# The second half's first norm and small delta factors emitted ahead of the first half's branches; six modulation units later, two of them beside the expert rows

## Chip, cores and metric

One core of a Trainium2 chip runs the whole program once. The metric is the device time of one execution in microseconds, and the number compared is the median of three executions. Times inside a run come from one profiled execution and are counted from the start of its span.

## What is computed

One transformer block on 512 tokens of width 1024, in float32: a modulation vector from the condition, a token mixer of two recurrent branches (HGRN2 and gated delta net), and a product-key expert layer with 16384 experts, of which each token takes 8 x 16. Cut to what matters here:

```python
mod = (cond @ ada_w[l] + ada_b[l])[:, None, :]
sh1, sc1, gt1, sh2, sc2, gt2 = jnp.split(mod, 6, axis=-1)
h = rmsnorm(x, norm1_g[l]) * (1.0 + sc1) + sh1
y = token_mixer(h, ...)          # projections, two recurrences, two gated branches, w_out
x = x + gt1 * y
h = rmsnorm(x, norm2_g[l]) * (1.0 + sc2) + sh2
x = x + gt2 * peer(h, ...)       # scores over all keys, top 16 per head, weighted sum of expert rows
return rmsnorm(x, final_g)
```

In the mixer `beta_raw` and `a_raw` (8 columns of the projection) give the small factors of the delta net: beta, the log decay and its cumulated exponentials.

## The kernel before

**Halves.** The 512 tokens go through the mixer in two halves of 256. A half is normed and transposed into `hh` and `hl` (`front_norm`, line 806, over `norm_t`, line 232): high and low parts, because every wide product is made of three float32r products (`mm3`, lines 202 to 204). Both lie in a pool with one buffer of each, so those of the second half can be written only when the last product that reads the first half's is done. `gdn_small` (line 262) then makes the small factors: 16 narrow products from `hh` and `hl` (lines 267 and 269), two transposes, and a chain of some 20 tiny DVE operations.

**Weights.** A projection unit is two loads of 512 KB on SP's queue (`half_unit`, line 191), each into one of four buffers named `raw`; ACT casts it to `whi` (line 197), DVE makes `wlo` (line 198), and 48 products on PE read them.

**Modulation units.** The modulation is made in 12 units of 512 columns (`ada_unit`, line 135). A unit loads 4 x 512 KB into the same four `raw` buffers (line 142), sums eight slices on DVE into `adac` (lines 146 and 152) and ends with a product on PE. Units 0 to 3 (shift and scale of the first norm) run at the start. Units 4 and 5 give the gate `gt1`, 6 to 9 shift and scale of the second norm, 10 and 11 the gate `gt2`. A gate's unit loads its bias row (`adar`, line 159), adds the product (line 161) and stores it in DRAM (line 162), from where it is read much later.

**Order of the mixer.** `mixers` (line 825) is a generator: convolutions and projections of the delta net, the inverses in steps of three, the HGRN2 projections, `hgrn_core`, then `gdn_seq` (line 456), the recurrence of the delta net, in four steps one after the other (two pairs of heads by two blocks of 128 tokens). For the first half the gate projections of all branches follow, then a head norm and `branch` for HGRN2 and for the delta net. `run(mixers(0, *h1), ar, ADA[1], ADA[0])` (line 972) puts modulation unit 4 and those after it between its steps: none for the first `ADA[0]` steps, then one after every `ADA[1]` steps, 6 and 2. After it come `front_norm` for the second half, four steps of `back0` (the output projection of the first half, `mix_out`, line 867), and `mixers(1)` with the rest of `back0` beside it.

**Expert layer.** Three token blocks go through dense products over all experts, the fourth through gathered expert rows. In `dense` (line 1181) item i is one block of 128 experts: `value_parts` (line 1109) loads 512 KB of values through the same `raw` buffers, `wlo` on DVE (line 1003), the 192 KB of scores `gr` from DRAM (line 1117), times the gates `g` (line 1121), split into `ah` and `al` (lines 1124, 1125); then 18 products into `y`. Every eighth item loads the next 1.5 MB of gates (line 1113). Scores of the first 32 items were made ahead. `gather_block` (line 1136) runs beside it, with `rows` gathered by GpSimd and summed on DVE.

**What sets the order.** The framework's scheduler orders the instructions of each engine, by the order of emission and a timeline that it assumes; each engine then runs its own list strictly in that order. What is written earlier gets precedence, but instructions far apart in the code lie side by side on an engine.

Of the kernel before, what the change touches and what calls it, by code (L numbers as in the profile page):

```python
# [11 lines left out]
F32 = mybir.dt.float32  # L12
# [8 lines left out]
P = 128  # L21
# [23 lines left out]
GB = 3  # L45
NGS = 5
NST = 4
ADA = (6, 2)
ND = 384
AHEAD = 32  # L50
LEAD = 3
# [15 lines left out]
def mixer_peer_kernel(ctx: ExitStack, tc: tile.TileContext, x, ws, ada, wba, vecs, rows, skt, uv, ut, out, dbg=None):  # L67
# [17 lines left out]
    def bank(tag):  # L85
        return (psh if tag == "hg" else ps).tile([P, 512], F32, tag=tag, name=tag, bufs=psb[tag])
# [4 lines left out]
    def w2(tag, shape=(P, 2, 256), dt=F32, bufs=1, name=None):  # L91
        pool = wka if tag in WKA else wkb if tag in WKB else wk
        return pool.tile(list(shape), dt, tag=tag, name=name or tag, bufs=bufs)
# [38 lines left out]
    a1 = cst.tile([P, KD], F32, name="a1")  # L132
    a2 = cst.tile([P, KD], F32, name="a2")

    def ada_unit(u, first=False):

        pp = bank("tr")
        acc = w2("ac", (P, 512), bufs=2, name="adac")
        parts = []
        for i in range(4):  # L140
            w = st.tile([P, 2, 512], F32, tag="raw", name="adaw")
            nc.sync.dma_start(w, ada[u, :, 2 * i:2 * i + 2])
            for a in range(2):
                kk = 2 * i + a
                if kk == 0:
                    nc.vector.tensor_scalar(acc, w[:, 0, :], cond[:, 0:1], None, op0=ALU.mult)
                elif first and a:
                    p = w2("gs", (P, 512), bufs=NGS, name="adap")
                    nc.scalar.mul(p, w[:, a, :], cond[:, kk:kk + 1])
                    parts.append(p)  # L150
                else:
                    nc.vector.scalar_tensor_tensor(acc, w[:, a, :], cond[:, kk:kk + 1], acc,
                                                   op0=ALU.mult, op1=ALU.add)
        parts.append(acc)
        if u // 2 in (2, 5):
            dst, o = (g1d, RW_B1) if u < 6 else (g2d, RW_B2)
            k = u % 2 * 512
            r = w2("ac", (P, 512), bufs=2, name="adar")
            nc.sync.dma_start(r, bass.AP(tensor=rows.tensor, offset=rows.offset + o + k, ap=[[0, P], [1, 512]]))
            nc.tensor.matmul(pp, ones, acc, start=True, stop=True)  # L160
            nc.vector.tensor_add(r, r, pp)
            nc.sync.dma_start(dst[:, k:k + 512], r)
            return
        for n, p in enumerate(parts):
            for c in range(4):
                nc.tensor.matmul(pp[:, c * P:(c + 1) * P], p[:, c * P:(c + 1) * P], ones, start=n + c == 0,
                                 stop=n == len(parts) - 1, skip_group_check=True)
        m = mod[:, 4 * u:4 * u + 4]
        nc.vector.tensor_add(m, pp.rearrange("p (c n) -> p c n", c=4)[:, :, 0],
                             vec[:, VC_ADAB + 4 * u:VC_ADAB + 4 * u + 4])  # L170
        if u // 2 in (1, 4):
            dst, g = (a1, VC_N1) if u < 6 else (a2, VC_N2)
            k = u % 2 * 4
            nc.vector.scalar_tensor_tensor(dst[:, k:k + 4], m, 1.0, vec[:, g + k:g + k + 4], op0=ALU.add, op1=ALU.mult)
# [443 lines left out]
    def gate_sig(p, gu, js, hh, hl):  # L618
        r = []
        for j in js:  # L620
            s = gate_tile(p, "gsig")
            nc.scalar.activation(s, proj_tm(gu + j, hh, hl), AF.Sigmoid)
            r.append(s)
            yield
        return r
# [164 lines left out]
                next(aux, None)  # L790

    def ada_rest():
        for u in range(4, 12):
            ada_unit(u)
            yield

# [25 lines left out]
                next(aux, None)  # L822
            yield

    def mixers(p, hh, hl):
        fac = gdn_small(hh, hl)
        yg = w2("yg", (P, 2, 512))
        yh = w2("yh", (P, 2, 512))
        loc = [gdn_pre(0, (yield from gdn_convs(0, fac, hh, hl)))]
# [14 lines left out]
        if p == 0:  # L844
            sg[0] = yield from gate_sig(p, U_GH, range(4), hh, hl)
            gg = yield from gate_proj(p, U_GG, RW_GDN, hh, hl)
            sg[1] = yield from gate_sig(p, U_GD, range(4), hh, hl)
        yhi, ylo = head_norm_t(yh, gh)
        if "yh" in dbg:
            nc.sync.dma_start(dbg["yh"].rearrange("(t p) c -> p t c", p=P)[:, 2 * p:2 * p + 2], yh)  # L850
        if p == 0:
            mg = [w2(n, name="mg") for n in ("hv", "att", "he", "rl")]
        else:
            y2 = w2("yh", (P, 2, 2, 256), name="mg2")
            mg = [y2[:, 0], y2[:, 1]] + [w2("ac", bufs=2, name="mg") for _ in range(2)]
# [68 lines left out]
    h1 = front_norm(0, xc)  # L924
# [44 lines left out]
    ar = ada_rest()  # L969
    RT = dict(side="right", reuse_waits="tile")  # L970
    with tc.tile_pool(name="g0", bufs=1, **RT) as early_gates:
        mg = run(mixers(0, *h1), ar, ADA[1], ADA[0])

    per = ctx.enter_context(tc.tile_pool(name="per", bufs=1, **RT))
    dhi = per.tile([P, KD, ND], F32R, name="dhi")
    dlo = per.tile([P, KD, ND], F32R, name="dlo")
    run(ar)
    h1 = front_norm(1, load_x(1))
    bk = back0(mg)
    for _ in range(4):  # L980
        next(bk)
    mg = run(mixers(1, *h1), bk)
    run(bk)
    c_wa.close()

# [195 lines left out]
    def dense():  # L1181
        for i in range(P - NEND):
            v = value_parts(i)
            for b in range(ND // P):
                for hf in range(2):
                    value_sum(i, b, hf, *v)
            if AHEAD <= i + LEAD < P:
                scores(i + LEAD)
            if i >= 20 or i % 2:
                yield  # L1190
            if i >= AHEAD - LEAD and i % 3 == 0:
                yield
# [84 lines left out]
```

## Time and profile before

| | us |
|---|---|
| median of 3 executions | 1919.0 |
| lowest and highest | 1909.81, 1921.65 |
| the profiled execution, whole | 1918.66 |
| its span | 1916.6 |
| PE (matmul) busy in the span | 1848.3 |
| DVE busy | 1565.6 |
| ACT busy | 966.8 |

The whole time of the profiled execution is 2.1 us more than its span and within 0.4 us of the median. PE is TensorE's matmuls, PEld its weight loads, DVE VectorE, ACT ScalarE, POOL GpSimd, SP the queue on which all plain loads and stores are issued. A row of a timeline gives start, duration, engine, line, operation and tiles, and in brackets the idle time of the engine just before and what ended it. PEclk is the granted clock of TensorE as a share of 2.4 GHz; 0.5 is 1.2 GHz. In order of time: modulation units 0 to 3 (to 37 us), the first half's mixer (to 317), the second half's with the rest of the first half beside it (to 700), routing, gates and early scores (to 954), then the dense expert layer to the end.

### The profile page before, as it was taken

What the parts mean: (1) busy time and instruction counts of PE and PEld (TensorE: products, weight loads), DVE (VectorE), ACT (ScalarE), POOL (GpSimd) and SP (SyncE); (2) the same over time, 40 slices, a digit from 0 to 9 for tenths busy, and PEclk for the clock granted to TensorE, in tenths of its full rate; (3) what the DMA queues carried; (4) which work ended last, traced back from release to release, by engine and by line L of the source; (5) the groups of instructions that cost most, each with busy time, mean ns of one, the idle gap of its engine ahead of it and who ended that gap; (6) DMA issues with size and microseconds to landing.
All of it is one profiled execution on the core that took longest, in us unless ns stands there. A gap on an engine that the chain in (4) does not pass through costs nothing.

```text
span 1916.6 us, 31296 instructions
## 1 busy us (share of the span) xinstructions
PE 1848.3 (96%) x11441; PEld 1709.3 (89%) x11441; DVE 1565.6 (82%) x3422; ACT 966.8 (50%) x1723; POOL 422.3 (22%) x433
## 2 busy tenths in 40 slices
PE   7989998999999899999999999999999999999997
PEld 6989887999989889999987799899899899899896
DVE  5989766889999989999755987878777778788755
ACT  5667544676655688788333333333333333333332
POOL 1010000000000587796100332221122222112100
PEclk9999998999999999999999999999999999999999
DMA  9556663543345555656897998888988998889843
GB/s 312 171 174 193 231 216 119 181 152 115 100 139 157 180 186 195 223 187 246 259 307 208 335 384 319 316 291 314 328 313 306 327 327 282 321 311 327 299 127 110
DMA packets 160521, 459.45 MB, mean 240 GB/s; under 512 B 12528, under 2 KB 78192, under 8 KB 140912
## 3 DMA queue, kind: packets, MB, share of 16 engines
q1 hardware_dynamic: 141936, 323.23, 51.3%
q0 software_dynamic: 18432, 134.23, 18.4%
q8 instruction: 90, 1.47, 0.3%
q14 instruction: 63, 0.52, 0.1%
HBM read 420.71 MB, written 36.70 MB: 239 GB/s over the span
## 4 chain that ended last, share of the span: by engine, by line
PE 81%; DVE 8%; ACT 4%; DMA 4%; POOL 2%; issue 1%; SPq 0%; DVEq 0%; POOLq 0%; ACTq 0%
PE y L203 9%; PE y L204 9%; PE y L202 9%; PE hg L203 9%; PE hg L202 9%; PE hg L204 9%; PE pj L203 6%; PE pj L204 6%; PE pj L202 6%; PE gd L1050 3%; DVE wlo L198 2%; POOL oj L1037 1%; DMA adaw<-in_ada 1%; DMA gr<-sd 1%; DMA raw<-in_ws 1%
## 5 line engine op out<-in xcount | busy, mean ns | idle before, releaser
L1003 DVE TENSOR_TENSOR wlo<-raw,whi 128x1024 fp32r<-128x1024 f32 x256 | 313.1, 1223 | 123.3 <-ACT whi L1002 120.6
L1002 ACT CAST whi<-raw 128x1024 fp32r<-128x1024 f32 x256 | 267.9, 1047 | 241.4 <-PE y L204 222.2
L202 PE MATMUL hg<-dlo,whi 128*128 128x384 f32 x1024 | 348.0, 340 | 1.5 <-ACT ga L1016 1.5
L203 PE MATMUL hg<-dhi,wlo 128*128 128x384 f32 x1024 | 348.1, 340 | 0.0
L204 PE MATMUL hg<-dhi,whi 128*128 128x384 f32 x1024 | 347.5, 339 | 0.0
L1141 POOL DMA_INDIRECT rows<-in_uv,ei x128 | 169.9, 1327 | 737.8 <-DVE acc L1149 571.3
L203 PE MATMUL y<-whi,al 128*128 128x512 f32 x768 | 304.7, 397 | 3.0 <-DVE al L1125 2.9
L204 PE MATMUL y<-whi,ah 128*128 128x512 f32 x768 | 304.4, 396 | 0.0
L202 PE MATMUL y<-wlo,ah 128*128 128x512 f32 x768 | 295.1, 396 | 0.0
L1037 POOL TENSOR_SCALAR oj<-iof,tj 128x128 f32<-128x128 f32 x256 | 213.3, 850 | 55.9 <-PE gd L1050 36.7
L198 DVE TENSOR_TENSOR wlo<-raw,whi 128x1024 fp32r<-128x1024 f32 x160 | 195.5, 1222 | 33.7 <-ACT whi L197 33.3
L197 ACT CAST whi<-raw 128x1024 fp32r<-128x1024 f32 x160 | 167.6, 1049 | 108.3 <-PE pj L204 66.2
L202 PEld LDWEIGHTS hg<-dlo,whi 128*128 128x128 f32 x1024 | 192.2, 188 | 6.3 <-ACT ga L1016 2.2
L1016 ACT ACTIVATE ga<-hg 128x384 f32<-128x384 f32 x128 | 63.0, 492 | 266.9 <-PE hg L204 266.8
L203 PEld LDWEIGHTS hg<-dhi,wlo 128*128 128x128 f32 x1024 | 192.2, 188 | 4.2
L204 PEld LDWEIGHTS hg<-dhi,whi 128*128 128x128 f32 x1024 | 192.2, 188 | 0.0
L203 PEld LDWEIGHTS y<-whi,al 128*128 128x128 f32 x768 | 144.6, 188 | 36.1 <-DVE al L1125 5.4
L204 PEld LDWEIGHTS y<-whi,ah 128*128 128x128 f32 x768 | 144.5, 188 | 34.7
L202 PEld LDWEIGHTS y<-wlo,ah 128*128 128x128 f32 x768 | 144.5, 188 | 31.2 <-ACT ah L1124 0.3
L1154 DVE SCALAR_TENSOR_TENSOR rows<-rows,h2g 128x1024 f32<-128x1024 f32 x128 | 153.9, 1220 | 0.4 <-DMA rows<-in_uv,ei 0.4
L204 PE MATMUL pj<-whi,hh 128*128 128x256 f32 x448 | 129.1, 288 | 0.0
L202 PE MATMUL pj<-wlo,hh 128*128 128x256 f32 x448 | 129.1, 288 | 0.0
(745 smaller groups left out, 3876.7 us busy)
## 6 DMA issues: line engine op xcount, KB each, us to landing
raw<-in_ws SPq DMA_DIRECT2D x160, 512.0 KB, 4.1
raw<-in_ut SPq DMA_DIRECT2D x128, 512.0 KB, 6.1
raw<-in_uv SPq DMA_DIRECT2D x128, 512.0 KB, 5.9
adaw<-in_ada SPq DMA_DIRECT2D x48, 512.0 KB, 4.8
gd<-stage SPq DMA_DIRECT2D x24, 1024.0 KB, 4.6
g<-gd SPq DMA_DIRECT2D x15, 1536.0 KB, 12.3
sd<-ga SPq DMA_DIRECT2D x32, 192.0 KB, 2.8
gr<-sd SPq DMA_DIRECT2D x32, 192.0 KB, 3.9
```

What stands on the lines that cost most here:

```text
L197: nc.scalar.copy(hi, w)
L198: nc.vector.tensor_sub(lo, w, hi)
L202: nc.tensor.matmul(o, lh, rl, start=start, stop=False, **kw)
L203: nc.tensor.matmul(o, ll, rh, start=False, stop=False, **kw)
L204: return nc.tensor.matmul(o, lh, rh, start=False, stop=stop, **kw)
L1002: nc.scalar.copy(hi, w)
L1003: nc.vector.tensor_sub(lo, w, hi)
L1016: nc.scalar.activation(a, o[:, :ND], AF.Gelu)
L1037: (nc.gpsimd if a < npool else nc.vector).tensor_scalar(oj4[:, a, :], iof, tj[:, t0 + a:t0 + a + 1], None, op0=ALU.is_equal)
L1050: last["pe"] = nc.tensor.matmul(pb4(pp, a), oj4[:, a, :], oi4[:, a, :], start=True, stop=True)
L1141: nc.gpsimd.indirect_dma_start(out=r[c], out_offset=None, in_=uv, in_offset=bass.IndirectOffsetOnAxis(ap=ei[:, c:c + 1], axis=0))
L1154: dot = nc.vector.scalar_tensor_tensor(u, u, 1.0, h2, op0=ALU.mult, op1=ALU.mult, accum_out=s)
```

## The change

- `ADA` becomes (12, 2): the units between the first half's steps begin after the twelfth step, and there are six of them (4 to 9).
- Units 10 and 11 are emitted in `dense`, after items 8 and 16, with `adac` and `adar` in the pool `d3` and the product in a bank named `hg`.
- `load_x(1)`, `front_norm(1)` and `gdn_small` of the second half are emitted inside `mixers(0)`, after the last gate projection and ahead of the head norms and branches. `mixers` takes the small factors as an argument.

The number of products, loads and DVE operations stays as it was.

```diff
-ADA = (6, 2)
+ADA = (12, 2)
...
-    def ada_unit(u, first=False):
-
-        pp = bank("tr")
-        acc = w2("ac", (P, 512), bufs=2, name="adac")
+    def ada_unit(u, first=False, pool=None):
+        def work(name):
+            return w2("ac", (P, 512), bufs=2, name=name) if pool is None else pool.tile([P, 512], F32, tag=name, name=name)
+
+        pp = bank("tr") if pool is None else None
+        acc = work("adac")
...
-            r = w2("ac", (P, 512), bufs=2, name="adar")
+            r = work("adar")
...
+            pp = bank("hg") if pp is None else pp
...
-        for u in range(4, 12):
+        for u in range(4, 10):
...
-    def mixers(p, hh, hl):
-        fac = gdn_small(hh, hl)
+    def mixers(p, hh, hl, fac, done=None):
...
             sg[1] = yield from gate_sig(p, U_GD, range(4), hh, hl)
+            done()
         yhi, ylo = head_norm_t(yh, gh)
...
-        mg = run(mixers(0, *h1), ar, ADA[1], ADA[0])
+        nxt = []
+
+        def next_half():
+            h = front_norm(1, load_x(1))
+            nxt.extend((*h, gdn_small(*h)))
+
+        mg = run(mixers(0, *h1, gdn_small(*h1), next_half), ar, ADA[1], ADA[0])
...
     run(ar)
-    h1 = front_norm(1, load_x(1))
     bk = back0(mg)
...
-    mg = run(mixers(1, *h1), bk)
+    mg = run(mixers(1, *nxt), bk)
...
             if AHEAD <= i + LEAD < P:
                 scores(i + LEAD)
+            if i in (8, 16):
+                ada_unit(10 + i // 16, pool=d3)
```

Three places show what the scheduler makes of it. Lines of the changed kernel are a few higher than those of before: 194 is 199, 142 is 146, 159 is 163, 162 is 167.

SP's queue in the first half, before, from the last loads of units 0 to 3 (the twelve `adaw` are three of them); `raw` are weights, `adaw` modulation weights:

```order
L142 DMA adaw<-in_ada 128x1024 x12
L194 DMA raw<-in_ws 128x1024 x3
...
L194 DMA raw<-in_ws 128x1024 x12
L142 DMA adaw<-in_ada 128x1024 x4
L194 DMA raw<-in_ws 128x1024 x4
L142 DMA adaw<-in_ada 128x1024 x4
L159 DMA adar<-in_rows 128x512
L162 DMA g1d<-adar 128x512
L159 DMA adar<-in_rows 128x512
L194 DMA raw<-in_ws 128x1024 x4
```

The same place now:

```order
L146 DMA adaw<-in_ada 128x1024 x12
L199 DMA raw<-in_ws 128x1024 x3
...
L199 DMA raw<-in_ws 128x1024 x24
L146 DMA adaw<-in_ada 128x1024 x2
L163 DMA adar<-in_rows 128x512
L146 DMA adaw<-in_ada 128x1024 x2
L199 DMA raw<-in_ws 128x1024 x4
L146 DMA adaw<-in_ada 128x1024 x3
L167 DMA g1d<-adar 128x512
```

Twelve weight loads (six units) that stood behind modulation units 4 to 6 now stand ahead of unit 4; from there on the units follow each other after every four weight loads, as before.

PE near the end of the first half, before: a step of the delta net's recurrence (lines 460, 467, 472, 478, 484, in this order in a step) among gate projections (`pj` from `hh` and `hl`), with the next step begun behind it:

```order
L203 MATMUL pj<-whi,hl 128x256
L467 MATMUL gd<-r,Xt 128x128 x2
L472 MATMUL gd<-gst,qT 128x128 x2
L204 MATMUL pj<-whi,hh 128x256
...
L614 MATMUL hg<-ident,yh 128x128 x8
L478 MATMUL gd<-z,kd 128x128 x2
L484 MATMUL gd<-z,aq 128x128 x2
L460 MATMUL gd<-gst,kT 128x128 x2
L202 MATMUL pj<-wlo,yhi 128x512 x3
```

Now, behind the first branch's last product (a step is lines 465, 472, 477, 483, 489; 272 and 274 are the narrow products of `gdn_small`, eight of each):

```order
L209 MATMUL pj<-whi,yhi 128x512
L465 MATMUL gd<-gst,kT 128x128 x2
L472 MATMUL gd<-r,Xt 128x128 x2
L477 MATMUL gd<-gst,qT 128x128 x2
L483 MATMUL gd<-z,kd 128x128 x2
L489 MATMUL gd<-z,aq 128x128 x2
...
L272 MATMUL gd<-hh,wb 16x256
L274 MATMUL gd<-hl,wb 8x256
...
L280 MATMUL gd<-ident,ba 128x16 x2
L619 MATMUL hg<-ident,yg 128x128 x8
```

Three of the four steps stand back to back, with no wide product between; the narrow products follow, and then the transposes of the delta net's output `yg`.

DVE in the dense stage, before, from item 8's `gr` (12010) to item 9's `al` (12045):

```order
L1121 TENSOR_TENSOR gr_12010<-gr_12010,g_12008 128x384
L1003 TENSOR_TENSOR wlo_12005<-raw_12002,whi_12004 128x1024
L1121 TENSOR_TENSOR gr_12041<-gr_12041,g_12008 128x384
L1125 TENSOR_TENSOR al_11959<-gr_11955,ah_11958 128x384
L1003 TENSOR_TENSOR wlo_12038<-raw_12035,whi_12037 128x1024
L1125 TENSOR_TENSOR al_12014<-gr_12010,ah_12013 128x384
...
L1125 TENSOR_TENSOR al_12045<-gr_12041,ah_12044 128x384
```

Now, from unit 10's third sum to item 9's `al` (12022; `wlo_12015` is item 9's too, `al_11968` item 8's):

```order
L156 SCALAR_TENSOR_TENSOR adac_11989<-adaw_11994,cond_104,adac_11989 128x512
L1014 TENSOR_TENSOR wlo_11959<-raw_11956,whi_11958 128x1024
...
L156 SCALAR_TENSOR_TENSOR adac_11989<-adaw_11998,cond_104,adac_11989 128x512 x2
L1136 TENSOR_TENSOR al_11968<-gr_11964,ah_11967 128x384
L156 SCALAR_TENSOR_TENSOR adac_11989<-adaw_12002,cond_104,adac_11989 128x512
L1132 TENSOR_TENSOR gr_12071<-gr_12071,g_11962 128x384
L156 SCALAR_TENSOR_TENSOR adac_11989<-adaw_12002,cond_104,adac_11989 128x512
L1014 TENSOR_TENSOR wlo_12015<-raw_12012,whi_12014 128x1024
L1136 TENSOR_TENSOR al_12022<-gr_12018,ah_12021 128x384
```

The low part of item 9's values now waits in DVE's list behind the unit's last sum, and with it behind the unit's last load.

## Rows read from the trace of the kernel before

**Rows 1.** The page, part 1: busy us, share of the span, instructions.

```profile
PE 1848.3 (96%) x11441; PEld 1709.3 (89%) x11441; DVE 1565.6 (82%) x3422; ACT 966.8 (50%) x1723; POOL 422.3 (22%) x433
```

**Rows 2.** Windows: stretch, length, busy of each engine (instructions), PEclk, DMA share, GB/s.

```profile
core 0: us, PE busy (x) PEld busy (x) DVE busy (x) ACT busy (x) POOL busy (x), PEclk, DMA share, GB/s
...
80.00:140.00 60.00, 52.42 (x370) 48.03 (x369) 50.17 (x109) 40.75 (x88) 6.07 (x5) 0.89 0.49 154
140.00:220.00 80.00, 78.34 (x677) 77.71 (x676) 72.13 (x132) 55.76 (x94) 0.00 (x0) 1.00 0.65 209
220.00:240.00 20.00, 16.15 (x112) 15.83 (x111) 15.29 (x27) 7.41 (x9) 2.07 (x1) 0.83 0.69 228
...
280.00:320.00 40.00, 31.24 (x150) 23.36 (x149) 29.15 (x69) 19.10 (x42) 3.04 (x3) 0.87 0.35 111
320.00:540.00 220.00, 220.00 (x1874) 218.56 (x1873) 202.18 (x632) 148.29 (x269) 9.78 (x7) 1.00 0.44 137
...
955.00:1045.00 90.00, 90.00 (x386) 72.35 (x385) 45.17 (x59) 31.93 (x44) 2.61 (x3) 1.00 0.83 267
```

**Rows 3.** Timeline of PE, narrow windows: four waits of the first half.

```profile
88.28 1.28 PE L518 MATMUL hg<-hq,hk 128*128 128x128 f32 x8 [2.70 <-ACT hq L503]
...
115.93 1.50 PE L355 MATMUL gd<-rl,gt 128*128 128x512 f32 x2 [2.67 <-DVE rl L353]
...
233.18 2.07 PE L442 MATMUL gd<-X,al 128*128 128x128 f32 x8 [3.85 <-ACT X L438]
...
292.49 2.59 PE L614 MATMUL hg<-ident,yg 128*128 128x128 f32 x8 [6.42 <-DVE yg L600]
```

**Rows 4.** Timeline of SP's queue, 66 to 125 us.

```profile
69.95 7.88 SPq L142 DMA_DIRECT2D adaw<-in_ada  x4
83.66 11.66 SPq L194 DMA_DIRECT2D raw<-in_ws  x4
97.74 7.49 SPq L142 DMA_DIRECT2D adaw<-in_ada  x4
...
119.60 3.66 SPq L194 DMA_DIRECT2D raw<-in_ws  x2
```

**Rows 5.** Instructions of the tile adaw: ns min/median/max, and its loads.

```profile
L152 DVE SCALAR_TENSOR_TENSOR adac<-adaw,cond,adac x68: 732/746/755, 11.3 to 249.6; 128x512 f32<-128x512 f32 x68
...
DMA to landing us min/median/max: 3.7/4.8/5.8
```

**Rows 6.** Timeline 264 to 273 us: a step of the recurrence among other work.

```profile
264.61 0.61 PE L460 MATMUL gd<-gst,kT 128*128 128x128 f32 x4
...
265.25 0.61 DVE L463 SCALAR_TENSOR_TENSOR r<-gd,neb,vr 128x128 f32<-128x128 f32 x2 [0.45 <-PE gd L460]
...
267.87 0.60 PE L467 MATMUL gd<-r,Xt 128*128 128x128 f32 x4
268.31 0.61 PE L472 MATMUL gd<-gst,qT 128*128 128x128 f32 x4
268.51 0.42 DVE L469 COPY z<-gd 128x256 f32<-128x256 f32 x1 [0.48 <-PE gd L467]
...
270.76 0.61 DVE L480 SCALAR_TENSOR_TENSOR gst<-gst,eb,gd 128x128 f32<-128x128 f32 x2 [1.83 <-PE gd L478]
```

**Rows 7.** Timelines of POOL and DVE, 284 to 298 us: the two norms.

```profile
289.37 1.64 POOL L126 TENSOR_TENSOR rsh<-rs,mhalf 128x8 f32<-128x8 f32 x1 [64.04 <-DVE rs L125]
...
291.81 0.16 DVE L240 TENSOR_REDUCE ssq<-ssq 128x2 f32<-128x8 f32 x1 [2.52 <-ACT junk L238]
```

**Rows 8.** Instructions of the tile mod: the norm's eight activations per half.

```profile
L254 ACT ACTIVATE h<-hg,mod,a x32: 544/563/598, 31.2 to 691.3; 128x256 f32<-128x256 f32 x32
```

**Rows 9.** Timeline of SP's queue, 1000 to 1013 us.

```profile
1001.69 0.37 SPq L1113 DMA_DIRECT2D g<-gd  x1
1002.26 5.02 SPq L1117 DMA_DIRECT2D gr<-sd  x1
1007.37 0.38 SPq L999 DMA_DIRECT2D raw<-in_uv  x1
```

**Rows 10.** Instructions of the tile raw, 955 to 1045 us: its loads.

```profile
DMA to landing us min/median/max: 3.9/4.0/11.2
```

**Rows 11.** Windows: a stretch with idle time on PE at full clock.

```profile
540.00:560.00 20.00, 17.66 (x131) 16.24 (x131) 18.70 (x73) 8.79 (x20) 1.64 (x1) 1.00 0.45 128
```

## The prediction

> **What bounds the kernel now.** I read the page's busy shares first: PE is busy 96% of the span [rows 1], so the time is PE's work, its holes, and what the clock takes away. The profiled execution took 1918.66 us and the median is 1919.0, so every sum below starts at 1918.66 and needs no correction. Within 1% (19 us) is about what a measurement of this kernel can tell from no change.
>
> Then the windows, to find the holes in the stretches that the change touches [rows 2]. From 80 to 140 us PE is busy 52.42 of 60 us at a granted clock of 0.89; from 220 to 240, 16.15 of 20 at 0.83; from 280 to 320, 31.24 of 40 at 0.87. Between them, 140 to 220 has 78.34 of 80 at full clock, and 320 to 540 is full, 220.00 of 220. The dense stage is full on PE too (90.00 of 90), with DVE at only 45.17. So what can be won lies in three places of the first half, and whatever is added to the dense stage must fit beside a PE that never waits.
>
> A window's loss has two parts: idle time, and busy time that runs at less than full clock, (1 − clock) × busy:
> - 80 to 140: 7.58 + 0.11 × 52.42 = 5.8, together 13.4 us.
> - 220 to 240: 3.85 + 0.17 × 16.15 = 2.7, together 6.6 us.
> - 280 to 320: 8.76 + 0.13 × 31.24 = 4.1, together 12.8 us.
>
> PE's timeline gives the waits behind these: 2.70 us for `hq`, 2.67 for `rl`, 3.85 for `X`, 6.42 for `yg` [rows 3]. They are short chains through ACT and DVE which projections would cover if their weights were there. SP's queue shows why they were not: four unit loads at 69.95, four weight loads at 83.66, four unit loads at 97.74 [rows 4]. From 69.95 to 97.74, 27.8 us, four weight loads came, which is two projections. A projection is 48 products, and a product takes 220.00 / 1874 = 0.117 us in the full stretch [rows 2], so two feed PE for 11.2 us of those 27.8.
>
> **Part by part.**
>
> *Units later (80 to 140).* Twelve more weight loads go ahead of unit 4, so the two blocks of unit loads in that stretch leave it, and DVE loses two units' 16 sums of 0.746 us there, 12 us [rows 5], in a stretch in which it is busy 50.17 of 60. With weights at hand the stretch should look like the next, 140 to 220, which loses 1.66 us in 80, or 1.2 in 60: 13.4 − 1.2 = 12.2. The chains of `hq` and `rl` stay, and I keep one short wait of about 1 us: −11. Bounds: −13.4 (all of it) and −4 (the two waits, 5.4 us, go, and alternation that begins within the stretch brings back a part).
>
> *The units that remain (220 to 240).* Six units still follow each other after every four weight loads, and two fewer have to end before the recurrence. I take away the wait of 3.85 and leave the clock: −4. Bounds −6.6 and 0; DVE is busy 15.29 of 20 there, so a wait for it may stay.
>
> *Norm, factors and recurrence (280 to 320).* This is what the emission moves. What goes: the wait for `yg` (6.42), before which the second half's squares on ACT stood; DVE itself waited 2.52 us for their `junk` [rows 7]. They now lie far earlier. What comes is a recurrence without cover. One step is a chain: product, `r`, product, `z`, product, `gst`, or 0.61 + 0.61 + 0.60 + 0.42 + 0.61 + 0.61 = 3.46 us [rows 6] (line 478's product counted like line 472's). PE issues five pairs in it, 0.44 us apart (267.87 to 268.31), 2.2 us. So a bare step leaves 1.3 us idle; three of them, 3.8. Behind the last step come the output's `yg` (0.42, as `z`), four squares (an estimate, 1.7, four of that size), small DVE work (0.6), the power on POOL (1.64 [rows 7]) and a scaling (0.42): 4.8 us, of which 16 narrow products cover 16 × 0.117 = 1.9, leaving 3.0. The norm's `hh` can be written only behind the last gate projection: eight activations of 0.563 us [rows 8] less eight transposes, 4.5 − 1.0 = 3.5. With the clock's 4.1 as now, the stretch would lose 3.8 + 3.0 + 3.5 + 4.1 = 14.4 instead of 12.8: +1.6. So I expect one long wait to be exchanged for many short ones, with no gain. Bounds: −8.8 (all idle goes) and +8 (a wait of 6.42 comes on top).
>
> Whether many short waits keep the clock down is open. The rows have waits of 2.70, 2.67, 3.85 and 6.42 us in windows whose clock is 0.89, 0.83 and 0.87, and a stretch (540 to 560) with 17.66 us busy of 20 and the clock at 1.00 [rows 2, 3, 11]. So 2.3 us of holes in 20 do not lower it; many holes with little work between them are in no row.
>
> The Trainium skill ("TensorE: Matmul & The Clock Gate", section "A second HAM failure mode: psum-queue depth-cycling") says that short idles between groups of products, if frequent enough, make the clock go back and forth. By that rule the bare recurrence and the narrow products would run at half clock from end to end; the sum it gives stands with the first rival.
>
> *Units 10 and 11 in the dense stage.* Their two products are moved, not added: 0. Their 16 sums, 16 × 0.746 = 12 us [rows 5], fit into DVE's 45 idle us of that stage. What can hurt is the order: the low part of item 9's values, and the same place at item 16, waits in DVE's list behind the unit's last sum, and so behind its last load. `raw` loads there land in 4.0 us as a rule, but one took 11.2 [rows 10], 7.2 late; SP itself was held 5.02 us at `gr` behind the issue of the 1.5 MB of gates `g` [rows 9]. Bounds: 0, and one such meeting in full, 7.2 + 5.0 = 12. Values are loaded some items ahead, so I take half of one hold: +2.5.
>
> *The rest, 320 to 954.* The same work with one norm fewer in it; 320 to 540 is full and can't gain. 0, ± 5 (a wait of `yg`'s kind more, or less).
>
> **Sum.** −11 − 4 + 1.6 + 2.5 = −10.9; 1918.66 − 10.9 = 1907.8, about 1908 us.
>
> **Rivals.**
>
> *First: the holes only move.* The six units still pass the same four `raw` buffers, and their alternation now meets the gate projections, the inverses' end and the recurrence. A second loss of the size of 220 to 240, +6.6 in place of −4, gives −11 + 6.6 + 1.6 + 2.5 = −0.3: 1918 us. For it: SP's alternating blocks [rows 4] go on unchanged, only later. Against it: 140 to 220, where units alternated too, lost 1.66 us only [rows 2]. The same sum comes from another mechanism: 16 narrow products and three steps of five pairs, all at half clock, double 1.9 + 6.6 = 8.5 us, of which the 4.1 already counted is a part, and the next products run slow with them for about as long as the stretch 220 to 240 paid, 2.7; 8.5 − 4.1 + 2.7 = 7, on −10.9, is −4: 1915 us. This is what the skill's rule above would do here.
>
> *Second: nearly all is kept.* The stretch 80 to 140 as full as the next (−12.2), 220 to 240 without loss (−6.6), the tail behind the recurrence and the clock's fall avoided (14.4 − 3.0 − 4.1 = 7.3 in place of 12.8, −5.5), nothing lost in the dense stage: −24.3, 1894 us. For it: the fullness of 140 to 220 and 320 to 540. Against it: a bare recurrence, which no row shows running full.
>
> *Third, slower: the dense stage stalls.* Each unit's last load falls behind the gates' 1.5 MB: 7.2 late, 5.0 held on SP, two sums 1.5, so 13.7 us, at item 9 and at item 16, and the clock falls with each (2.7, as in 220 to 240): 2 × 16.4 = 33 on −13.4 for the other terms, 1938 us. It decides from the point at which the two stalls together exceed 13.4, some 6.7 us each. For it: the landing of 11.2 and the hold of 5.02 [rows 9, 10]. Against it: every other item has no such load in its way, PE never waited there, and value loads run ahead.
>
> That the change does not do what it says can be left out: the lists of SP, PE and DVE show it.
>
> **How the numbers follow.** Forecast 0.48 (its own range 1900 to 1916), holes that only move 0.24 (1912 to 1924), nearly all kept 0.20 (1888 to 1900), stalls in the dense stage 0.08 (1925 to 1945). The range 1892 to 1926 leaves out about a third of the second rival and nearly all of the third, some 0.15, and a little for what I did not see. Faster by over 1% (below 1899.5) takes nearly all of the second rival and little of the forecast: 0.22. Slower by over 1% (above 1937.9) is half of the third rival and some unforeseen: 0.07. Within 1%: 0.71.
>
> **What would show it.** Right: SP issues 24 weight loads before unit 4; PE's idle time from 80 to 140 is 1 to 3 us and its clock there 0.95 or more; the place of the 6.42 us wait holds three bare steps with idle times near 1.3 us; PE stays full in the dense stage but for 1 to 3 us about items 9 and 16; DVE's waits there are for `adaw`. Wrong: waits near 3.85 us at `X` or in the gates with a clock below 0.9 (first rival), a recurrence at half clock (its second form), a first half that ends 20 us or more earlier (second), PE waits over 6 us at `y` in the dense stage (third).

## The result, and the profile after

The changed kernel takes 1901.15 us (median of 6 executions, 1898.40 to 1902.23) against 1915.3 for the kernel before (6 executions, 1909.81 to 1921.65): ratio 0.9928, interval 0.9911 to 0.9945, 0.7% faster. The forecast was 1908. The profiled execution took 1898.62 us (span 1896.7), 20 us less than the profiled one of before; the medians are 14 apart. Of the 6 us between these two figures, 3.4 are the old kernel's, whose profiled execution, 1918.66, lies near the top of its spread, and 2.5 the new one's, whose profiled execution lies below its median. Single executions carry a few microseconds of that kind in every comparison of traces below; the comparisons of kernels rest on ratios.

The page, part 1, of the kernel after (busy us, share, instructions); compare [rows 1]:

```profile
PE 1844.5 (97%) x11441; PEld 1708.1 (90%) x11441; DVE 1565.9 (83%) x3422; ACT 972.9 (51%) x1726; POOL 421.5 (22%) x433
```

The work is the same. What changed is where PE waits. Windows of after, with the columns of [rows 2]:

```profile
80.00:140.00 60.00, 57.56 (x472) 55.39 (x471) 49.38 (x103) 48.22 (x89) 3.30 (x3) 1.00 0.53 168
140.00:220.00 80.00, 78.12 (x667) 76.95 (x666) 73.64 (x139) 63.88 (x118) 3.30 (x3) 1.00 0.63 200
220.00:240.00 20.00, 20.00 (x174) 20.00 (x173) 17.37 (x34) 8.79 (x15) 2.07 (x1) 1.00 0.80 268
240.00:280.00 40.00, 34.28 (x196) 28.20 (x194) 26.29 (x67) 16.91 (x45) 3.36 (x2) 0.91 0.37 120
280.00:320.00 40.00, 36.58 (x226) 33.35 (x225) 26.43 (x57) 16.61 (x26) 0.53 (x1) 0.87 0.37 119
...
955.00:1045.00 90.00, 88.15 (x371) 69.19 (x370) 59.88 (x89) 29.84 (x43) 3.15 (x2) 1.00 0.88 281
```

A window's loss, as in the prediction, is its idle time plus (1 − clock) × busy. From 80 to 140 us it has gone from 13.3 us (13.4 in the prediction's rounding) to 2.4, and from 220 to 240 it has gone altogether. But 240 to 280, which was nearly full before, now loses 5.7 idle and 3.1 by the clock. SP's queue shows why the early stretch is full (start, duration, line, transfer, count):

```profile
61.80 42.59 SPq L199 DMA_DIRECT2D raw<-in_ws  x14
108.55 3.60 SPq L146 DMA_DIRECT2D adaw<-in_ada  x2
```

Weight loads run on until 104 us with no unit load between them, and the first unit load stands at 108.55; before, unit loads stood at 69.95 and 97.74 [rows 4]. PE's timeline around the recurrence shows what took the place of the long wait for `yg` [rows 3]. Lines 465, 472, 483 and 489 are the recurrence's, 619 the transposes:

```profile
254.00 0.61 PE L489 MATMUL gd<-z,aq 128*128 128x128 f32 x4
...
261.22 0.75 PE L472 MATMUL gd<-r,Xt 128*128 128x128 f32 x4 [1.49 <-DVE r L468]
...
262.95 0.85 PE L483 MATMUL gd<-z,kd 128*128 128x128 f32 x4 [0.53 <-DVE z L474]
...
266.17 1.22 PE L472 MATMUL gd<-r,Xt 128*128 128x128 f32 x4 [0.45 <-DVE r L468]
...
268.96 1.23 PE L489 MATMUL gd<-z,aq 128*128 128x128 f32 x4
...
278.14 0.33 PE L619 MATMUL hg<-ident,yg 128*128 128x128 f32 x1 [1.53 <-DVE yg L605]
...
298.31 0.80 PE L207 MATMUL pj<-wlo,dhi 128*128 128x256 f32 x2 [3.27 <-ACT dhi L620]
```

Three things are to be seen. The bare steps wait 0.4 to 1.5 us at a time for DVE. The same four passes of line 489 take 0.61 us at 254 and 1.23 at 268.96: the clock has gone to its lower level, 1.2 GHz, with no wait above 1.49 us ahead of it. And the output projection has a wait of 3.27 us for `dhi` that the kernel before did not have.

### The profile page after: what moved, and what is told of

Its sections match the earlier page's. It is cut to its first block, busy times and chain, and to the rows that moved or that the text cites. A ratio compares the mean times of both kernels' runs of the same rounds, so it can differ in the third digit from the quotient of the medians.

```text
span 1896.7 us, 31316 instructions
## 1 busy us (share of the span) xinstructions
PE 1844.5 (97%) x11441; PEld 1708.1 (90%) x11441; DVE 1565.9 (83%) x3422; ACT 972.9 (51%) x1726; POOL 421.5 (22%) x433
## 4 chain that ended last, share of the span: by engine, by line
PE 91%; ACT 3%; DMA 2%; DVE 2%; POOL 1%; issue 1%; SPq 0%; DVEq 0%; POOLq 0%; ACTq 0%
PE hg L208 9%; PE hg L209 9%; PE hg L207 9%; PE y L208 9%; PE y L209 9%; PE y L207 9%; PE pj L207 8%; PE pj L208 8%; PE pj L209 8%; PE gd L1061 3%; PE hg L543 1%; POOL oj L1048 1%; PE gd L453 1%; PE gd L447 1%; PE pj L1061 1%; DMA adaw<-in_ada 1%
## 5 line engine op out<-in xcount | busy, mean ns | idle before, releaser
L1048 POOL TENSOR_SCALAR oj<-iof,tj 128x128 f32<-128x128 f32 x256 | 218.7, 871 | 49.7 <-PE gd L1061 32.6
```

Of the source, the lines that this page charges most:

```text
L1048: (nc.gpsimd if a < npool else nc.vector).tensor_scalar(oj4[:, a, :], iof, tj[:, t0 + a:t0 + a + 1], None, op0=ALU.is_equal)
```

## The experiments

**How a stretch is read.** As in the prediction, a window's loss is its idle time plus (1 − clock) × busy, worked out from the window's row. Three stretches are compared: 80 to 140 us (where the first units were), 140 to 240, and 240 to 320 (recurrence, second branch, start of the output projection). The stretches are fixed in time, and the same work lies earlier in a faster kernel (the transposes of `yg` begin at 292 us in before and at 278 in after). The table has the kernel before, profiled twice, and all other combinations of the three parts of the change:

| kernel | starts after step | units 10, 11 | norm | median us | ratio, 95% | loss 80:140 | 140:240 | 240:320 |
|---|---|---|---|---|---|---|---|---|
| before | 6 | first half | late | 1915.3 | 1 | 13.3 | 8.3 | 13.9 |
| before_again | 6 | first half | late | 1915.52 | 1.0001 (0.9988 to 1.0015) | 13.8 | 4.4 | 13.9 |
| ada_only | 12 | first half | late | 1917.0 | 1.0009 (0.9996 to 1.0022) | 1.8 | 3.7 | 26.1 |
| dense_only | 6 | dense | late | 1909.19 | 0.9969 (0.9954 to 0.9984) | 14.1 | 1.7 | 13.9 |
| front_only | 6 | first half | early | 1906.55 | 0.9967 (0.9949 to 0.9985) | 11.0 | 5.5 | 9.9 |
| no_front | 12 | dense | late | 1902.62 | 0.9937 (0.9915 to 0.9959) | 2.7 | 2.2 | 16.5 |
| ada_front | 12 | first half | early | 1911.36 | 0.9978 (0.9963 to 0.9993) | 1.4 | 2.1 | 20.4 |
| dense_front | 6 | dense | early | 1908.52 | 0.9969 (0.9955 to 0.9984) | 14.0 | 4.0 | 6.8 |
| after | 12 | dense | early | 1901.15 | 0.9928 (0.9911 to 0.9945) | 2.4 | 1.9 | 16.9 |

Ratios are to runs of the kernel before on the same chip. The losses are of one profiled execution each, and one clock fall more or less moves them by about 3 us.

**before_again.** No edit: the kernel before, profiled once more.

> The kernel before, unchanged, profiled once more. Theory: the clock falls at the waits for hq, rl, X and yg (near 89, 116, 232 and 290 us of the span) come from the order of the work and return in every execution; the spread of the times of before (1909.8 to 1921.7) then has another source, such as the start; time 1910 to 1921, the same four falls. Rival: the falls differ from one execution to the next, and the spread is theirs: of the four one or two are missing, and the profiled time is some 6 to 8 us lower than the first profile's 1918.7.

The time is that of before. The windows from 80 to 140 and from 280 to 320 us have their clocks of 0.89 and 0.87 again; the fall at 220 to 240 us did not come back. Its window (columns as above):

```profile
220.00:240.00 20.00, 16.85 (x137) 15.97 (x136) 17.54 (x31) 7.42 (x9) 2.07 (x1) 1.00 0.72 248
```

PE idles 3.15 us there at a clock of 1.00; in the first profile it was 3.85 at 0.83 [rows 2]. So falls do differ between executions (the rival). The two profiled executions differ by 6.2 us: 3.9 of them in the window 140 to 240 and 2.7 in the early dense stage, where PE idles 2.88 us from 955 to 1075 us in the first and 0.16 in the second. What makes the executions differ stays open.

**ada_only**: the later start alone.

```diff
-ADA = (6, 2)
+ADA = (12, 2)
```

> Only the step from which the modulation units begin is changed, 12 for 6; all eight units stay between the first half's steps, and norm, small factors and dense stage are as before. Theory (the gain is the emptied stretch from 80 to 140 us): that stretch loses 2 to 3 us instead of 13.4, and since the two units more have to go somewhere before the first half ends, the loss near 220 to 240 us stays: about -10 us, 1905 on a before of 1915. Rival (the holes only move): eight units behind the twelfth step are too many, a wait of 4 us or more with a clock fall appears between 140 and 300 us for each one saved, and the time is within 3 us of before.

No gain: the rival. The early stretch is emptied as forecast, 13.3 to 1.8, and the recurrence's stretch grows by about the same amount, 13.9 to 26.1. The window of ada_only there:

```profile
240.00:320.00 80.00, 60.52 (x334) 49.20 (x333) 54.97 (x119) 30.39 (x69) 2.92 (x3) 0.89 0.50 167
```

Two waits on PE's timeline in that stretch:

```profile
270.65 0.71 PE L465 MATMUL gd<-gst,kT 128*128 128x128 f32 x4 [2.15 <-DVE gst L485]
...
276.69 1.22 PE L483 MATMUL gd<-z,kd 128*128 128x128 f32 x4 [2.72 <-DVE z L474]
```

DVE's timeline at the second of them (line 156 is a unit's sum, 474 the copy that the step waits for):

```profile
275.55 0.75 DVE L156 SCALAR_TENSOR_TENSOR adac<-adaw,cond,adac 128x512 f32<-128x512 f32 x1 [2.79 <-DMA adaw<-in_ada]
276.22 0.42 DVE L474 COPY z<-gd 128x256 f32<-128x256 f32 x1
```

The copy of `z` stands in DVE's list behind a sum that waits 2.79 us for its load. The last two of eight units now meet the recurrence, and the recurrence stands bare, because the gate projections that used to lie between its steps have gone ahead: the last product from the first half's `hh` starts at 243.6 us and the recurrence's first at 243.0, where before they start at 269.1 and 241.6.

**dense_only**: only units 10 and 11 moved.

```diff
-        for u in range(4, 12):
+        for u in range(4, 10):
...
+            if i in (8, 16):
+                ada_unit(10 + i // 16, pool=d3)
```

> Only units 10 and 11 are moved into the dense stage; the other six begin after step 6 as before, norm and small factors as before. Theory (their place in the first half is worth something by itself): the wait for X and the clock fall near 232 us go, the dense stage pays about 0.6 us: -3 to -5 us, 1910 to 1912 on a before of 1915. Rival (it only pays when the units also begin later): the emptied place is taken by the same waits, within 2 us of before.

The theory, and a little more than it said: 0.9969, some 6 us. The window 140 to 240 loses 1.7 us in place of 8.3 and 4.4 in the two profiles of before; the other two stretches are as they were.

**front_only**: only the norm and the small factors moved.

```diff
+            done()
...
-    h1 = front_norm(1, load_x(1))
...
-    mg = run(mixers(1, *h1), bk)
+    mg = run(mixers(1, *nxt), bk)
```

> Only the emission of the second half's norm and small factors ahead of the branches; modulation units as before (eight, from step 6 on). Theory (one long wait for many short ones): the wait of 6.4 us for yg goes, the bare recurrence and a wait of about 3 us for dhi come, with the clock down for some 17 us in place of 10: +1 to +4 us, 1916 to 1919 on a before of 1915; the losses at 80 to 140 and 220 to 240 us stay as before. Rival (the emission is worth a good part of the gain): -5 us or better, 1910 or less.

The rival: 6 us faster by the ratio, where the theory had 1 to 4 slower. The window of the recurrence is fuller than before:

```profile
240.00:320.00 80.00, 73.06 (x488) 65.97 (x487) 58.69 (x130) 36.21 (x68) 3.81 (x3) 0.96 0.55 178
```

The wait for `yg` is gone, and with the units where they were the steps still have gate projections between them. The early norm does not bare the recurrence. The wait for `dhi` is here too, 3.79 us. Of the 6 us, 4.0 are in this stretch (13.9 to 9.9).

**no_front**: `ADA = (12, 2)` and the dense units, without the early norm.

> Both changes to the modulation units (begin after step 12, units 10 and 11 in the dense stage), without the early norm and small factors. Theory: -11 (80 to 140 us), -6.6 (220 to 240 us), +0.6 in the dense stage, the wait for yg of 6.4 us with its clock fall stays: -15 to -17 us, 1899 on a before of 1915, so 2 us or so faster than the whole change. Rival: the early norm carries part of the gain, and this kernel is 4 us or more slower than the whole change, 1905 or above.

0.9937: between the two. Its recurrence is bare too (16.5 us lost from 240 to 320), with the norm at its old place; and `yg` waits 4.36 us. The early norm on top is worth 0.9937 to 0.9928, which the intervals do not tell from nothing.

**dense_front**: the whole change with `ADA = (6, 2)`.

> The whole change but for the start of the units, which stays after step 6. Theory (the early norm is worth 8 us where gate projections still stand between the recurrence's steps, and beginning later takes them away): the losses from 80 to 140 us stay (about 13 us), the steps of the recurrence are covered by projections, idle time among them under 2 us: 1903 to 1906 on a before of 1915, 2 to 5 us slower than the whole change. Rival (the parts simply add, the later start being worth nothing as it was alone): 1901 or less, no slower than the whole change.

The theory, a little worse: 1908.52, about 7 us above the whole change. The recurrence's stretch is the fullest of all, level with every_1 below; the window of dense_front:

```profile
240.00:320.00 80.00, 74.65 (x522) 68.22 (x521) 55.64 (x124) 40.63 (x74) 3.80 (x3) 0.98 0.47 148
```

It gains 10 us on after there and loses 11.6 from 80 to 140 and 2 from 140 to 240. That is 3.6 of the 8.8 us between the two profiled executions. The rest is from 540 to 700 us (the second half's end): 19.8 us lost against 14.5 in after. The windows of after, dense_front and ada_front, in this order:

```profile
540.00:700.00 160.00, 150.03 (x1112) 141.39 (x1112) 149.27 (x394) 104.29 (x180) 73.69 (x88) 0.97 0.53 172
540.00:700.00 160.00, 147.62 (x1069) 139.32 (x1068) 142.27 (x355) 100.83 (x176) 62.27 (x79) 0.95 0.51 167
540.00:700.00 160.00, 148.54 (x1037) 138.83 (x1036) 141.29 (x355) 97.46 (x173) 61.94 (x77) 0.91 0.51 162
```

No edit is made there. Whether the earlier part of the order brings this loss, or chance does, is not shown.

**ada_front**: the whole change with all eight units in the first half.

> The whole change but for the two units in the dense stage: eight units, from step 12 on. Theory (units 10 and 11 then fall into the recurrence, whose small DVE operations wait behind sums that wait for loads): waits of 1.4 to 2.7 us between its products as with the later start alone, and the time is 8 us or more above the whole change: 1909 to 1915 on a before of 1915. Rival (the parts simply add: 0 for the later start, -8 for the early norm): 1907 and no long waits among the steps.

The theory's time and waits: 1911.36, 10 us above the whole change, with waits of 2.13 and 1.66 us among the steps. But its cause carries only a part: from 240 to 320 it loses 20.4 us, 3.5 more than after, while from 540 to 700 us it loses 24.8 against 14.5 (the last row above). Why it loses there is not shown.

**start_9**: a start between the two.

```diff
-ADA = (12, 2)
+ADA = (9, 2)
```

> The whole change with the units beginning after step 9 instead of 12 (eight weight loads fewer ahead of unit 4): in the lists, one step of the recurrence has gate projections between, the second the norm's transposes, the third the first branch's products, and only the last stands bare. Theory (the later start gains in 80 to 140 us and loses in the recurrence, and both can be had in part): 80 to 140 us loses 4 to 8 us, idle time and half clock around the recurrence are some 5 us less than in the whole change: 1898 to 1901, no slower than it. Rival (the early stretch is worth more than the cover): 1903 to 1907.

The rival's time: 1907.21. The early stretch loses 4.5, the next 4.7, and the recurrence's 16.8, as much as in after: the half cover bought nothing. The last step and the tail behind it are still bare, with waits of 1.48, 0.53 and 1.34 us.

**every_1**: a unit after every step from the twelfth.

```diff
-ADA = (12, 2)
+ADA = (12, 1)
```

> The whole change with a modulation unit after every step from the twelfth on, instead of every second: two weight loads (one projection) between units instead of four. In the lists gate projections now stand between the products of all steps of the recurrence, and the first branch ahead of the transposes of yg. Theory (the order trades supply against cover: what is covered later must be fed through the same four buffers): the recurrence costs under 3 us in idle time, but each of the five projections between units waits for its weights, 3 MB at the 200 to 270 GB/s of these stretches being 11 to 15 us against 5.6 us of products: 5 to 9 us lost each, with clock falls, 1920 or more. Rival (the bare recurrence is what the later start costs, and the loads run ahead far enough): 1893 to 1898, some 5 us faster than the whole change.

The direction of the theory, less in size: 1910.66, where it had 1920 or more. The recurrence is covered (6.8 us lost from 240 to 320), and the stretch ahead of it is starved. Its window:

```profile
140.00:240.00 100.00, 87.10 (x691) 83.89 (x690) 83.61 (x166) 62.83 (x128) 5.61 (x4) 0.95 0.59 182
```

SP's queue in that stretch:

```profile
169.08 10.35 SPq L146 DMA_DIRECT2D adaw<-in_ada  x4
179.76 6.17 SPq L199 DMA_DIRECT2D raw<-in_ws  x2
190.27 8.71 SPq L146 DMA_DIRECT2D adaw<-in_ada  x4
```

A unit and the two weight loads behind it take 21.2 us (169.08 to 190.27), for one projection.

**steps_early**: the first pair's two steps emitted before the second pair's inverse is finished.

```diff
+        gdn_seq(0, fac, loc[0], yg)
         for hp in range(2):
...
-            gdn_seq(hp, fac, loc[hp], yg)
+            if hp:
+                gdn_seq(hp, fac, loc[hp], yg)
```

> The whole change, and the two recurrence steps of the first pair of heads emitted before the second pair's inverse is finished (their PSUM bank is the inverse's, and is taken in order of emission). In the list the two steps now have gate projections between their products, and two bare steps stand instead of three. Theory (bare steps cost idle time and hold the clock down): idle and half clock from the first bare step to the second branch shrink from about 14 us by 2 to 4 us, 1897 to 1899 on the whole change's 1901. Rival (the second pair's inverse, which now ends behind the first branch, is late instead): a new wait of 2 us or more for X or Xt, time as the whole change or above, 1901 to 1906.

The stretch 240 to 320 loses 13.0 us instead of 16.9, but not by the theory's cause: 3.5 of the 3.9 us are the clock's (0.94 for 0.89) and 0.4 idle time, and first_apart below, with its three bare steps, has 12.5 us and the same 0.94. From 140 to 240 it loses 4.0 instead of 1.9. The time is not better: 1903.71, 0.9946 (0.9927 to 0.9965). No wait of 2 us for `X` or `Xt` appeared, so it is not the rival's reason either. Its profiled execution loses 8.1 us from 700 to 1060 us against 3.8 in after, a stretch that the edit does not touch; that stretch varies from 2.9 (first_apart) to 8.3 (every_1) among kernels with the same work there, so this need not be the edit's.

**steps_bank**: the recurrence's products in another PSUM bank.

```diff
-            pk = bank("gd")
+            pk = bank("hg")
```

and the same for the four other tiles of `gdn_seq`.

> The whole change, and the recurrence's products in the PSUM bank hg instead of gd, which the inverse and the narrow products use. In the list two steps have gate projections between them, and the norm's transposes, the narrow products and the first branch stand between the last step and the transposes of yg. Theory (what stands bare costs, here the tail behind the recurrence): the wait of 1.5 us for yg goes, the steps' waits shrink by a third, -2 to -4 us, 1897 to 1899 on the whole change's 1901. Rival (hgrn's products and the inverse, which share hg, are pushed back and stand bare in turn): a run of 36 small products without cover, waits of 1 to 3 us there, 1903 or above.

The rival, and dearer than it said: 1933.33, 1.0105 (1.0080 to 1.0131). HGRN2's own products were pushed behind and stood bare, with six waits of 1.55 or 1.56 us in 18 us. Three of them on PE's timeline of steps_bank:

```profile
250.62 1.13 PE L543 MATMUL hg<-he 128*128 128x128 f32 x8 [1.56 <-DVE he L535]
253.30 2.05 PE L543 MATMUL hg<-he 128*128 128x128 f32 x8 [1.56 <-DVE he L535]
256.90 2.05 PE L543 MATMUL hg<-he 128*128 128x128 f32 x8 [1.55 <-DVE he L535]
```

The eight products take 1.13 us in the first row and 2.05 in the next: the clock falls to 1.2 GHz between them. The second half's recurrence uses that bank too, and from 540 to 700 us this kernel loses 25.5 us against 14.5 in after.

**first_apart**: the first quarter of the output projection's operands in memory of its own.

```diff
-        yield from back(0, mg, (dhi[:, :, P:], dlo[:, :, P:]), hh, hl)
+        scr = [Split(wka.tile([P, 2, 256], F32R, tag=n, name=n), d[:, :, P:]) for n, d in (("fhi", dhi), ("flo", dlo))]
+        yield from back(0, mg, scr, hh, hl)
```

`Split` hands out the tile of its own for the first two of eight row blocks and the old place for the rest.

> The whole change, and the first quarter of the output projection's operands (high and low part, 4 KB of a partition) in memory of its own instead of the pool that takes over the memory of the first half's gates. Theory (the new wait of 3.27 us for dhi is the wait for DVE's last product with a gate, since dhi lies where the gates lay; before, the norm of the second half covered it): ACT's first cast no longer waits for that product, the wait shrinks to 1.5 us or less in one piece, and with it perhaps the clock fall behind it (3.4 us): -1.5 to -5 us against the whole change, 1896 to 1900 on its 1901. Rival (the cast waits for the transposes and for DVE's casts of weights anyway): the wait stays near 3 us, time as the whole change.

The reading of the wait is right. In after, ACT's first cast waits for DVE's last product with a gate, as ACT's timeline has it:

```profile
297.67 1.07 ACT L620 CAST dhi<-hg 128x512 fp32r<-128x512 f32 x2 [2.42 <-DVE mg L654]
```

In first_apart the first cast does not wait, only the next one does:

```profile
294.98 0.58 ACT L620 CAST fhi<-hg 128x512 fp32r<-128x512 f32 x1
298.08 0.58 ACT L620 CAST dhi<-hg 128x512 fp32r<-128x512 f32 x1 [2.52 <-DVE mg L654]
```

PE's wait of 3.27 becomes two on the timeline of first_apart:

```profile
295.61 0.51 PE L207 MATMUL pj<-wlo,fhi 128*128 128x256 f32 x2 [0.75 <-ACT fhi L620]
297.72 1.12 PE L619 MATMUL hg<-ident,mg 128*128 128x128 f32 x4 [1.60 <-DVE flo L621]
```

That is 0.9 us less, and the time is level with the whole change, 1902.71, 0.9935 (0.9911 to 0.9959). Its stretch 240 to 320 loses 12.5 us where after loses 16.9. Of that, 3.1 us are the clock fall in the recurrence, ahead of what the edit touches, which this execution does not have (its rows are in the next section). No kernel of the study is clearly faster than the whole change; no_front, first_apart and steps_early cannot be told from it.

## Why the prediction was right, and where it was not

**Time and sign.** 1908 was forecast, 0.57% below before; 0.72% was measured. The starting point was the profiled execution and the median of three; over six executions before is 3.4 us lower than the 1918.66 used, and −10.9 from there is 1904.4. Runs of this kernel also tell more than the prediction took for granted ("within 1%"): the interval of the ratio is 0.17% to either side.

**80 to 140 us: −11.** By the windows −10.9. Right in place, cause and size: weight loads with no unit between them, no wait of PE for `hq` or `rl` from 80 to 140 us. What the step did not say is that this gain cannot be had by itself: ada_only has it and is no faster.

**220 to 240 us: −4.** The window has gone from 6.6 to 0, but before_again pays only its 3.15 idle us there, so −3 to −7 in single executions. No single edit is what it takes: PE is busy 20.00 of 20 us there in dense_only (two units fewer, the old start) and in ada_front (all eight units, the later start).

**280 to 320 us: +1.6, for the early norm. This is the step that failed.** The prediction put the bare recurrence on the norm's move: "What comes is a recurrence without cover." The runs show otherwise. The recurrence is bare in no_front and ada_only, which have the norm at its old place, and covered in front_only and dense_front, which have it early. It is the later start that bares it: the first half's projections then run ahead of it, and none is left to lie between its steps. With the later start the last product from the first half's `hh` starts at 239 to 244 us (after, no_front, ada_only, ada_front), with the old one at 261 to 269 (before, dense_only, front_only, dense_front); the recurrence's first product starts at 235 to 247 in all eight. So the later start gives back in the recurrence what it gains early (ada_only: 11.5 gained, 12.2 lost), and the early norm is a gain of its own: 0.9967 alone. On top of no_front (0.9937) it brings less, 0.9928. A part of the difference is the wait for `yg`, which the early norm saves: 6.42 us in before and dense_only, where the recurrence is covered, and 4.36 in ada_only and no_front, where it is not.

That the stretch came out near the forecast all the same (+1.6 forecast, +3.0 from 240 to 320) is luck: a cost put down to the wrong edit, and terms that missed in both directions.

Within the stretch the terms compare like this. The step's waits: 3.8 forecast; 1.49 + 0.53 + 0.45 of the rows above and two smaller ones, about 3.0. The tail behind the last step: 3.0 forecast, 1.53 before the first transposes and 0.9 in smaller pieces. The norm's activations behind the last gate projection: 3.5 forecast, and the one wait of PE for its `h` is 0.24. The wait for `dhi`: not forecast, 3.27. It stands in front_only, ada_front and dense_front too (3.40 to 3.80 us) and in none of the kernels with the norm at its old place. The prediction had the norm's products as a cost and did not ask what they had been hiding: at their old place they filled the time in which DVE finished the second branch, and `dhi` lies in the memory of the gates that DVE still read. The clock: 4.1 forecast, (1 − 0.91) × 34.28 + (1 − 0.87) × 36.58 = 7.8 measured over 240 to 320. By windows of 2 us, 3.1 of it lie in the recurrence, 1.6 behind the wait for `yg` and 3.0 behind the wait for `dhi`.

**The clock under many short waits.** The prediction left this open, and it stays open. In after the row at 266.17 has 1.22 us for what takes 0.61 at 2.4 GHz, after waits of 1.49, 0.53 and 0.45 us with narrow work between. In first_apart the recurrence has the same waits in the same order, and runs at full clock to its end (granted clock 1.00 from 260 to 276 us):

```profile
262.25 0.75 PE L472 MATMUL gd<-r,Xt 128*128 128x128 f32 x4 [1.49 <-DVE r L468]
...
263.97 0.71 PE L483 MATMUL gd<-z,kd 128*128 128x128 f32 x4 [0.53 <-DVE z L474]
...
266.54 0.75 PE L472 MATMUL gd<-r,Xt 128*128 128x128 f32 x4 [0.45 <-DVE r L468]
```

The bare steps of no_front ran at full clock too, behind waits of 1.20 and 0.44 us. The Trainium skill ("TensorE: Matmul & The Clock Gate", section "A second HAM failure mode: psum-queue depth-cycling") tells of a kernel in which frequent short idles between groups of products made the clock go back and forth. In after and in steps_bank the clock fell behind such idles, as the section has it; in the recurrences of first_apart and no_front it did not. The prediction made of the section a recurrence at half clock from end to end. That did not come: in after the half clock lasted from about 263 to 270 us, about half of the bare steps and narrow products.

**Dense stage: +2.5.** Sized too high: PE idles 2.88 us from 955 to 1075 us before and 1.85 in after. The new waits of DVE there are for `adaw`, as forecast (6.0 us in three waits), but PE is full from 940 to 1020 us, while the units' loads, sums and products run. Waits of PE in the early dense stage (what waited for what: sum, times, longest), before from 955 to 1075 us:

```profile
PE y L203 <- DVE al L1125: 2.9, 3, 1.2
```

After, from 955 to 1060 us:

```profile
PE y L208 <- DVE al L1136: 1.8, 2, 1.1
```

These waits are not the units'. In both kernels the longest stands behind a load of scores `gr` that SP held behind the gates (7.39 us at 1036.54 in before). In after, on the timelines of SP, DVE and PE:

```profile
1019.45 5.65 SPq L1128 DMA_DIRECT2D gr<-sd  x1
...
1029.44 0.56 DVE L1132 TENSOR_TENSOR gr<-gr,g 128x384 f32<-128x384 f32 x1 [6.41 <-DMA gr<-sd]
...
1030.52 0.50 PE L208 MATMUL y<-whi,al 128*128 128x512 f32 x1 [1.12 <-DVE al L1136]
```

The prediction's window for "PE never waited there" ended at 1045, just ahead of them. The two products of the units take 2.0 us of PE. The holds on which the slower rival stood came (SP held 4.09 and 5.26 us at the units' loads, one of which took 9.8 us to land) and did no harm to PE.

**The rest, 320 to 954 us: 0 ± 5.** Within its bounds: from 320 to 540 us after loses 1.4 us where before loses nothing, from 540 to 700 us it loses 14.5 for 17.6, and from 700 to 955 it loses 2.0 for 4.2. What brings this is not shown.

**The rivals.** "The holes only move" is what the later start does alone; in the profiled execution of the whole change it still gives back 3.0 of the 11 us (13.9 to 16.9 from 240 to 320); "nearly all is kept" fell with the bare recurrence; the dense stall did not come. The whole kept its gain because units 10 and 11 leave the place into which the holes would have moved: from ada_only, 1.0009, the dense units alone make 0.9937. The early norm alone makes 0.9978 of it (ada_front), and on top of the dense units its part is within the intervals.

## What to carry to other kernels

Moving loads or side work away from a starved stretch also moves the work that used to wait there, and that work may have been the cover of a chain further on: before crediting the gain, look in the new order at what now stands between the steps of each serial chain. When an edit takes work from a place, ask what that work was hiding (here a memory reuse that nobody had waited for), not only what it cost. And edits that each move holes are to be measured in all combinations: here the later start, worth nothing alone, is worth about 6 us on top of the moved units (dense_only to no_front) and about 8 on top of both other edits (dense_front to after).

## What was not expected of the hardware

The same wait does not always bring the clock down: at 220 to 240 us 3.85 idle us went with a clock of 0.83 in one execution of the kernel before and 3.15 with 1.00 in another, while in after a chain of waits of at most 1.49 us was followed by 1.2 GHz, and the same chain in first_apart by full clock.
